# A hybrid decoder block on one core: x tiles in one transfer each, first squares on two engines, six banks for the first transposes, the first weight cast on two engines, head bias rows loaded first

## The chip, the cores and the metric

The kernel runs on one core of a Trainium2 chip. A core has five engines that run side by side, each through its own instructions in order: TensorE (PE in the profile, its weight loads PEld), VectorE (DVE), ScalarE (ACT), GpSimd (POOL) and SyncE (SP), which here issues most of the DMA transfers. They wait for each other and for transfers through semaphores. Matrix products are written to PSUM, in banks of 128 partitions by 512 float32; everything else lies in SBUF. The metric is device time in microseconds (us) for one execution; 0.3% of this kernel is 2.4 us.

## The reference

One block on x of 512 rows by 1024 columns, float32:

```python
h = rmsnorm(x, norm1_g)
z = h @ w_in + b_in                      # 1024 x 6656
z_glu, z_rx, z_rg, z_ga, z_gb = split(z)
u = glu(z_glu); u = causal_depthwise_conv(u, 31 taps); u = silu(layernorm(u))
y_a = u @ conv_w_out + conv_b_out
xb = causal_depthwise_conv(z_rx, 4 taps)
hb = rg_lru(xb, lru_wa, lru_ba, lru_wx, lru_bx, lru_lambda)   # 16 heads of 80
y_b = (hb * gelu(z_rg)) @ lru_w_out
x = x + (sigmoid(z_ga) * y_a + sigmoid(z_gb) * y_b) @ w_mix_out
h = rmsnorm(x, norm2_g)
x = x + (silu(h @ ffn_w1) * (h @ ffn_w3)) @ ffn_w2
return rmsnorm(x, norm_f_g)
```

What matters here is the beginning: the root-mean-square norm of x, its transposition, the first products with w_in, and the small parameters (biases, gains, conv taps) that the later steps read as one column per channel.

## The kernel before

Every product is made of three, in the format that the profile calls fp32r: an operand v is split into h (v cast) and l (v - h), and h·h, h·l and l·h are summed. `split_to` makes both parts: a cast, by default on ACT, and a subtraction (`sub`, L118) on DVE or POOL. A weight chunk is 128 x 1024: `load_chunk` (L147) loads it into a `raw` tile, and `emit_chunk` (L166) splits it into an `hl` tile, low part on POOL for most of the w_in chunks.

The first stage is written out by hand for PE, ACT, DVE and SP (`manual_schedule`, L647); POOL's order follows the program. It goes:

- SP loads x as eight tiles of 128 rows by 512 columns (`load_x`, L494): x0 and x1 in two halves each, then the rows of norm1_g and b_in (`load_rows`, L487), two weight chunks, x2 and x3, two more chunks, the other parameter rows (eleven loads) and, last, the head bias rows (`load_head_rows`, L482). Each of SP's loads signals one of eight semaphores in turn and waits until the load eight before it has landed.
- `norm1_rows(t)`: ACT squares each half of tile t and sums along the row (L559, L565), each with a read of the accumulator; DVE puts in mean and epsilon (L560); ACT takes the root (L566); DVE inverts it (L567) and scales both halves (L614).
- `turn_rows(t)`: PE turns the eight 128 x 128 blocks of a tile (L594) into four PSUM banks, block c into bank c mod 4; x0 and x1 fill one set of banks together, x2 and x3 the next. A bank is read only when PE has written all that goes into it.
- `rows_turned(c0, c1)`: PE turns parameter rows into columns, and DVE copies these to `par` (L528). The first call does norm1_g and b_in; the second, later one all others and the head bias rows, which ACT halves into `bh` (L524). In that second call the head rows come first, `bh` next, the other rows after.
- `turned_parts`: for each block, ACT makes h (`h10h` to `h17h`, L602) with the gain as scale, DVE the low part (`h10l` to `h17l`, L603).
- `early_mm`: the first products. `early_mm(0, 0)` (L636) takes h10h, h10l, h11h ... with the high weights first, and the low weights from the eleventh product on.

The first chunk's cast is on DVE (the `vec.tensor_copy` in L166), its low part on POOL. `load_head_rows` clears its tile on POOL (L480) before the loads; POOL reaches that after the low parts of chunks 0, 2 and 3. After the first stage two ACT instructions (L716) halve 24 of the bias columns; in ACT's order they stand before h10h.

SBUF tiles come from pools: `long` (63 slots of 128 x 512), `raws`, `hls`, and `wsums`, three buffers of 128 x 1024 that the FFN weight sums use later. PSUM has two pools, six banks (`bank`) and two (`bank2`).

Of the kernel before, what the change touches and what calls it, by code (L numbers as in the profile page):

```python
# [85 lines left out]
def tile_block(ctx, tc, a, out):  # L86
# [19 lines left out]
    def bank(name):  # L106
        return psum.tile([P, T], F32, tag="mm", name=name)
# [12 lines left out]
    def split_to(h, l, full, eng, copy=act.copy):  # L120

        copy(h, full)  # L122
        last = sub(eng, l, full, h.bitcast(F32))
        if eng is pool_e:
            newest["sub"] = last.ins
        return h, l

    def split(name, full, eng, p_=None, copy=act.copy):
        p_ = p_ or pairt(name)
        return split_to(*p_, full, eng, copy)  # L130
# [19 lines left out]
    def emit_chunk():  # L150
        key, src, kt, cols, where, lo, after = chunks[emitted[0]]
        if emitted[0] not in loaded_raw:
            load_chunk(emitted[0])
        raw = loaded_raw.pop(emitted[0])
        emitted[0] += 1
        n = kt * cols
        rv = raw[:, :n]
        if where == "gate":
            hl = hls.tile([P, 2, 1024], F32R, tag="hl", name=f"hl_{key}")
            h = hl[:, 0, :n]  # L160
            after(rv, h)
# [314 lines left out]

    heads_b = longt("rowsh")

    def load_head_rows():
        pool_e.memset(heads_b[: 2 * NH, :P], 0.0)  # L480
        for g, name in enumerate(("lru_ba", "lru_bx")):
            nc.sync.dma_start(heads_b[g * NH : (g + 1) * NH, :HB], a[name][0].rearrange("(h p) -> h p", p=HB))  # L482

# [3 lines left out]
        nc.sync.dma_start(rowt[b][r : r + m, :P], src)  # L487

    x_nat = a["x"].rearrange("b (t p) d -> p (b t) d", p=P)
    xt = [[longt(f"x{t}{h}") for h in range(2)] for t in range(NT)]  # L490

    def load_x(t):
        for h in range(2):
            nc.sync.dma_start(xt[t][h], x_nat[:, t, h * T : (h + 1) * T])  # L494

# [22 lines left out]

    def rows_turned(c0, c1):
        pt = bank2(f"par_ps{c0}")  # L520
        if c0:
            at = T - 2 * NH
            pe.transpose(pt[:, at:], heads_b[: 2 * NH, :P], ident[: 2 * NH, : 2 * NH])
            act.activation(bh, pt[:HB, at:], AF.Copy, scale=0.5)  # L524
        for c in range(c0, c1, P):
            m = min(P, c1 - c)
            pe.transpose(pt[:, c - c0 : c - c0 + m], rowt[row_at(c)[0]][:m, :P], ident[:m, :m])
        vec.tensor_copy(par[:, c0:c1], pt[:, : c1 - c0])  # L528

    def pc(name, i):  # L530
        return par[:, col[name] + i : col[name] + i + 1]
# [44 lines left out]
    def turn_half(name, rows, gname, dest, hf, bk, some):  # L576
# [10 lines left out]
            last = vec.scalar_tensor_tensor(out=l, in0=ps[:, :256], scalar=g, in1=h.bitcast(F32), op0=ALU.mult, op1=ALU.subtract)  # L587
        return last_h.ins, last.ins

    def turn_rows(t, ps):  # L590

        for c in range(ND):
            at = 256 * (c // 4) + P * (t % 2)
            pe.transpose(ps[c % 4][:, at : at + P], xt[t][c // 4][:, (c % 4) * P : (c % 4 + 1) * P], ident)  # L594

    def turned_parts(hf, ps):
        cs = slice(hf * 256, hf * 256 + 256)
        for c in range(ND):
            g, at = pc("norm1_g", c), 256 * (c // 4)
            p_ = ps[c % 4][:, at : at + 256]  # L600
            h, l = (v[:, cs] for v in h1p[c])
            act.activation(h, p_, AF.Copy, scale=g)  # L602
            vec.scalar_tensor_tensor(out=l, in0=p_, scalar=g, in1=h.bitcast(F32), op0=ALU.mult, op1=ALU.subtract)  # L603
# [6 lines left out]
    def norm1_rows(t, between=lambda: None):  # L610
        junk = [shortt(f"n1j{t}{h}") for h in range(2)]
        r = rstd_of(xt[t], junk)
        for h in range(2):
            vec.tensor_scalar(out=xt[t][h], in0=xt[t][h], scalar1=r, scalar2=None, op0=ALU.mult)  # L614
            if h == 0:
                between()

    HALVES = [slice(0, 256), slice(256, 512)]
    EARLY = 2
# [3 lines left out]
    def early_mm(i, hf):  # L623
        m = EARLY_IN[i]
        if hf == 0:
            early.append((m, w_tiles(f"in{m}", ND, 0), bank(f"z{m}")))
        _, ws, ps = early[i]
        if (i, hf) == (0, 0):

            order = [(m, c) for c in range(5) for m in (0, 1)]  # L630
            order += [(2, 0), (2, 1), (0, 5), (1, 5), (2, 2), (2, 3), (0, 6), (1, 6), (2, 4), (2, 5), (0, 7), (2, 6), (2, 7), (1, 7)]
            xs = parts_of(h1p, HALVES[0])
            for n, (m, c) in enumerate(order):
                (wh, wl), (xh, xl) = ws[c], xs[c]
                l, r = ((wh, xh), (wh, xl), (wl, xh))[m]
                pe.matmul(ps[:, HALVES[0]], l, r, start=n == 0, stop=n == len(order) - 1)  # L636
            return
        mm3(ps[:, HALVES[hf]], ws, parts_of(h1p, HALVES[hf]), lo_last=hf == 0)
# [71 lines left out]

    def b_in(m):
        return pc("b_in", m)

    for m, n in ((GLU, 16), (GB, 8)):
        cols = par[:, col["b_in"] + m : col["b_in"] + m + n]
        act.activation(cols, cols, AF.Copy, scale=0.5)  # L716

    ready = {m: ps for m, _, ps in early}

# [873 lines left out]
```

## Time and profile before

| | us |
|---|---|
| median of 3 runs | 793.22 |
| lowest, highest | 792.25, 794.7 |
| profiled execution | 793.44 |
| its span, first to last instruction | 791.7 |
| PE busy in the span | 780.2 |
| DVE, ACT, POOL busy | 678.0, 475.0, 358.2 |

A row of the timeline gives start, length, engine, line of the kernel, operation, the tiles out<-in, the shape and a count; in brackets stands how long the engine sat idle before it and what ended that. "SPq" is an instruction that issues a transfer. A row of the lists of groups gives, after the count, the busy time in us, the mean of one in ns and the idle time before.

### The profile page before, as it was taken

The page shows a single profiled execution, that of the slowest core. Times are in us where ns is not written, and L with a number is a line of the kernel's source. Part 1 is how long each engine was busy: PE and PEld are TensorE (multiplying, and loading weights), DVE is VectorE, ACT ScalarE, POOL GpSimd, SP SyncE. Part 2 cuts the span into 40 slices and gives each one's busy share as a digit, 9 for nine tenths or more (in the row PEclk, how much of TensorE's full clock was granted, in tenths as well). Part 3 has the DMA queues.
Part 4 walks back from the last instruction along what each step waited for, and adds up shares of the span by engine and source line. Part 5 has one row for each costly group of instructions (what it writes and reads, how often), then busy time and mean ns, then how long its engine had stood idle before and what let it go on. Part 6 is the DMA issues. An engine that isn't in the chain of part 4 may idle for free.

```text
span 791.7 us, 12476 instructions
## 1 busy us (share of the span) xinstructions
PE 780.2 (99%) x4319; PEld 679.4 (86%) x4319; DVE 678.0 (86%) x1059; ACT 475.0 (60%) x697; POOL 358.2 (45%) x350
## 2 busy tenths in 40 slices
PE   8999999999999999999999999999999999999996
PEld 7888888888888888888887798999999999888885
DVE  5389998887989996999799969897877789999957
ACT  7444678966686866565234666544455546556743
POOL 2367877887788999645550481112322222000000
PEclk9999999999999999999999999999999999999999
DMA  7555999989979978989987896578988889878652
GB/s 218 148 162 169 257 257 259 250 233 288 261 224 300 298 226 266 292 276 286 335 276 247 245 284 208 181 250 290 331 304 300 300 300 292 258 240 260 207 172 107
DMA packets 192261, 199.04 MB, mean 251 GB/s; under 512 B 15278, under 2 KB 153926, under 8 KB 192198
## 3 DMA queue, kind: packets, MB, share of 16 engines
q1 hardware_dynamic: 183093, 166.52, 70.1%
q0 software_dynamic: 8960, 31.46, 11.7%
q8 instruction: 34, 0.56, 0.3%
q14 instruction: 30, 0.24, 0.1%
q10 hardware_dynamic: 144, 0.26, 0.1%
HBM read 146.30 MB, written 38.80 MB: 234 GB/s over the span
## 4 chain that ended last, share of the span: by engine, by line
PE 81%; DVE 10%; DMA 4%; ACT 3%; issue 2%; SPq 0%; DVEq 0%; ACTq 0%
PE z L543 36%; PE fr L1347 24%; PE or L1119 13%; PE f L543 3%; PE g L945 2%; PE yb L543 1%; DMA raw_mxt<-mxt 1%; PE fr L1391 1%; DVE hl_co L118 1%; DMA raw_co<-in_conv_w_out_dram 1%; DVE mxws L118 1%; DVE hl_lo L118 1%; DVE hl_mxb L118 1%; DVE sga L1185 1%; DMA mxws<-in_w_mix_out_dram 1%
## 5 line engine op out<-in xcount | busy, mean ns | idle before, releaser
L745 DVE SCALAR_TENSOR_TENSOR cv<-u,par,cv 128x507 f32<-128x507 f32 (+15 forms) x240 | 162.6, 734 | 1.8 <-ACT cv L741 0.9
L118 POOL TENSOR_TENSOR hl_in<-raw_in,hl_in 128x1024 fp32r<-128x1024 f32 x51 | 123.5, 2432 | 51.2 <-ACT hl_in L122 34.5
L118 POOL TENSOR_TENSOR fws<-fws 128x256 f32<-128x256 f32 x120 | 98.3, 821 | 82.0 <-DMA fws<-in_ffn_w_dram 76.0
L389 POOL DMA_DIRECT2D ot<-fwso x21 | 15.4, 733 | 164.7 <-DVE fwso L118 156.4
L1347 PE MATMUL fr<-hs_0h,hl_ft 128*128 128x256 f32 x320 | 59.2, 283 | 0.0
L122 ACT CAST hl_in<-raw_in 128x1024 fp32r<-128x1024 f32 x51 | 52.9, 1050 | 8.4 <-DMA raw_in<-in_w_in_dram 8.4
L118 DVE TENSOR_TENSOR hl_ft<-raw_ft,hl_ft 128x1024 fp32r<-128x1024 f32 x39 | 47.6, 1220 | 6.3 <-ACT hl_ft L122 6.3
L1347 PEld LDWEIGHTS fr<-hs_0h,hl_ft 128*128 128x128 f32 x320 | 50.6, 192 | 0.0
L122 ACT CAST hl_ft<-raw_ft 128x1024 fp32r<-128x1024 f32 x40 | 41.6, 1048 | 13.8 <-PE fr L1347 6.9
L118 DVE TENSOR_TENSOR hl_fb<-raw_fb,hl_fb 128x1024 fp32r<-128x1024 f32 x30 | 37.0, 1232 | 11.2 <-ACT hl_fb L122 11.1
L1347 PE MATMUL fr<-hs_0l,hl_ft 128*128 128x256 f32 x160 | 45.3, 283 | 0.0
L122 ACT CAST hl_fb<-raw_fb 128x1024 fp32r<-128x1024 f32 x30 | 31.6, 1052 | 17.7 <-PE fr L1347 9.1
L543 PE MATMUL z<-h10h,hl_in 128*128 128x512 f32 (+1 forms) x108 | 41.1, 382 | 0.0
L543 PE MATMUL z<-h13h,hl_in 128*128 128x512 f32 (+1 forms) x108 | 40.8, 379 | 0.0
L543 PE MATMUL z<-h14h,hl_in 128*128 128x512 f32 (+1 forms) x108 | 40.8, 379 | 0.0
L543 PE MATMUL z<-h15h,hl_in 128*128 128x512 f32 (+1 forms) x108 | 40.8, 379 | 0.0
L543 PE MATMUL z<-h16h,hl_in 128*128 128x512 f32 (+1 forms) x108 | 40.8, 379 | 0.0
L543 PE MATMUL z<-h11h,hl_in 128*128 128x512 f32 (+1 forms) x108 | 40.8, 379 | 0.0
L543 PE MATMUL z<-h12h,hl_in 128*128 128x512 f32 (+1 forms) x108 | 40.8, 379 | 0.0
L543 PE MATMUL z<-h17h,hl_in 128*128 128x512 f32 (+1 forms) x108 | 40.8, 379 | 0.0
L122 ACT CAST hl_ob<-raw_ob 128x1024 fp32r<-128x1024 f32 (+1 forms) x23 | 23.4, 1018 | 22.9 <-PE or L1119 14.2
L383 POOL TENSOR_TENSOR fws<-fws 128x256 f32<-128x256 f32 x40 | 32.5, 813 | 3.0
(906 smaller groups left out, 2590.9 us busy)
## 6 DMA issues: line engine op xcount, KB each, us to landing
raw_in<-in_w_in_dram SPq DMA_DIRECT2D x52, 512.0 KB
fws<-in_ffn_w_dram SPq DMA_DIRECT2D x40, 512.0 KB
raw_ft<-fs SPq DMA_DIRECT2D x34, 512.0 KB
fs<-fws SPq DMA_DIRECT2D x21, 512.0 KB
ot<-fwso POOLq DMA_DIRECT2D x21, 512.0 KB, 6.0
fwso<-in_ffn_w_dram POOLq DMA_DIRECT2D x40, 256.0 KB, 7.4
fs<-fws POOLq DMA_DIRECT2D x19, 512.0 KB, 5.1
raw_ob<-in_ffn_w_dram SPq DMA_DIRECT2D x33, 256.0 KB
```

The costliest lines, as they stand in the source:

```text
L118: return eng.tensor_tensor(out=o, in0=x, in1=y, op=ALU.subtract)
L122: copy(h, full)
L383: eng.tensor_tensor(out=q11, in0=q22, in1=q11, op=ALU.add)
L389: return queue.dma_start(dest, raw.rearrange("p (m n) -> p m n", n=256))
L543: pe.matmul(ps, l, r, start=i == 0, stop=i == n - 1)
L745: vec.scalar_tensor_tensor(out=acc[:, s:], in0=u[c][:, : T - s], scalar=dw(c, s), in1=acc[:, s:], op0=ALU.mult, op1=ALU.add)
L945: pe.matmul(ps[:HB], head_chunk[0][:ROWS_G, g, h % 2, m, :], ext[h][m][:ROWS_G], start=m == 0, stop=m == 1)
L1119: pe.matmul(banks[i], l_[:, ts], r_, start=start and n == 0, stop=stop and n == 2, skip_group_check=again)
L1185: vec.scalar_tensor_tensor(out=o, in0=ps, scalar=pc("conv_b_out", j), in1=o, op0=ALU.add, op1=ALU.mult)
L1347: pe.matmul(ps[:, HALVES[i]], lw[:, c, :], rx_, start=not (again or i or c or m), stop=bool(i and c == 3 and m == 2), skip_group_check=True,)
L1391: pe.matmul(self.r4[:, HALVES[i]], lw, rx_, start=not (i or c or m), stop=bool(i and c == 3 and m == 2), skip_group_check=True)
```

## The change

It has six edits, all in the first stage. They shift the line numbers of what follows, so a line number here is always one of the kernel before.

1. x0, x1 and x2 are loaded by one transfer each, of 128 x 1024, into the three `wsums` buffers. x3 stays in two halves.
2. For x0 and x1, `first_sums` squares the left half on ACT and the right half on DVE, by a fused multiply-and-sum whose start value and scale put in epsilon and mean; the root then takes both sums. The order on DVE is: sum of x0, scaling of x0's left half, sum of x1, scaling of x0's right half, scaling of x1's halves.
3. The first transposes go to six banks (five of one pool, one of the other); blocks 0 and 3 share a bank, and so do 4 and 7, and PE turns the blocks in the order 0, 3, 1, 2, 4, 7, 5, 6. The first parameter rows are turned between x0's transposes and x1's, and their columns copied on ACT instead of DVE.
4. The first weight chunk is cast half by ACT, before h10h, and half by POOL, before its low part.
5. The clearing for the head bias rows is POOL's first work after the constants, their loads stand before the other eleven, they are turned after the other rows, and `bh` is made last.
6. The scaling of bias columns stands behind the first product and x2's root on ACT.

After the first stage all engines have the same instructions in the same order as before.

```diff
+    def copy_halves(h, full):
+        act.copy(h[:, :T], full[:, :T])
+        pool_e.tensor_copy(h[:, T:], full[:, T:])
...
-            h, l = split_to(hl[:, 0, :n], hl[:, 1, :n], rv, lo, act.copy if emitted[0] > 1 else vec.tensor_copy)
+            h, l = split_to(hl[:, 0, :n], hl[:, 1, :n], rv, lo, act.copy if emitted[0] > 1 else copy_halves)
...
+    pool_e.memset(heads_b[: 2 * NH, :P], 0.0)
+
     def load_head_rows():
-        pool_e.memset(heads_b[: 2 * NH, :P], 0.0)
...
-    xt = [[longt(f"x{t}{h}") for h in range(2)] for t in range(NT)]
+    wide = [wsums.tile([P, 1024], F32, tag="wsum", name=f"x{t}") for t in range(PIECES)]
+    xt = [[w[:, :T], w[:, T:]] for w in wide] + [[longt(f"x{t}{h}") for h in range(2)] for t in range(PIECES, NT)]
 
     def load_x(t):
+        if t < PIECES:
+            nc.sync.dma_start(wide[t], x_nat[:, t, :])
+            return
...
         pt = bank2(f"par_ps{c0}")
-        if c0:
-            at = T - 2 * NH
-            pe.transpose(pt[:, at:], heads_b[: 2 * NH, :P], ident[: 2 * NH, : 2 * NH])
-            act.activation(bh, pt[:HB, at:], AF.Copy, scale=0.5)
         for c in range(c0, c1, P):
             m = min(P, c1 - c)
             pe.transpose(pt[:, c - c0 : c - c0 + m], rowt[row_at(c)[0]][:m, :P], ident[:m, :m])
-        vec.tensor_copy(par[:, c0:c1], pt[:, : c1 - c0])
+        at = T - 2 * NH
+        if c0:
+            pe.transpose(pt[:, at:], heads_b[: 2 * NH, :P], ident[: 2 * NH, : 2 * NH])
+        (vec.tensor_copy if c0 else act.copy)(par[:, c0:c1], pt[:, : c1 - c0])
+        if c0:
+            act.activation(bh, pt[:HB, at:], AF.Copy, scale=0.5)
...
+    def spot(c, ps):
+        return ((c % 4, c // 4 * 256), ((0, 1, 2, 0, 3, 4, 5, 3)[c], c in (3, 7) and 256))[len(ps) == 6]
+
     def turn_rows(t, ps):
-        for c in range(ND):
-            at = 256 * (c // 4) + P * (t % 2)
-            pe.transpose(ps[c % 4][:, at : at + P], xt[t][c // 4][:, (c % 4) * P : (c % 4 + 1) * P], ident)
+        for c in (range(ND), (0, 3, 1, 2, 4, 7, 5, 6))[len(ps) == 6]:
+            b, at = spot(c, ps)
+            at += P * (t % 2)
+            pe.transpose(ps[b][:, at : at + P], xt[t][c // 4][:, (c % 4) * P : (c % 4 + 1) * P], ident)
...
+    def first_sums(t):
+        junk = [shortt(f"n1j{t}{h}") for h in range(2)]
...
+        act.activation(junk[0], xt[t][0], AF.Square, accum_out=ss[:, 0:1])
+        vec.tensor_tensor_reduce(out=junk[1], in0=xt[t][1], in1=xt[t][1], scale=1.0 / D, scalar=EPS, op0=ALU.mult, op1=ALU.add, accum_out=ss[:, 1:2])
+        act.activation(r, ss[:, 0:1], AF.Sqrt, scale=1.0 / D, bias=ss[:, 1:2])
+        return r
...
-        turned = [bank(f"tx0{q}") for q in range(4)]
-        norm1_rows(0)
+        turned = [(bank if q < 5 else bank2)(f"tx0{q}") for q in range(6)]
+        r0 = first_sums(0)
+        vec.reciprocal(r0, r0)
+        scale_half(0, 0, r0)
+        r1 = first_sums(1)
+        scale_half(0, 1, r0)
         turn_rows(0, turned)
-        norm1_rows(1, lambda: rows_turned(0, n_first))
+        vec.reciprocal(r1, r1)
+        scale_half(1, 0, r1)
+        rows_turned(0, n_first)
+        scale_half(1, 1, r1)
         emit_to(1)
         turn_rows(1, turned)
         turned_parts(0, turned)
...
         norm1_rows(2)
         early_mm(0, 0)
+        for m, n in ((GLU, 16), (GB, 8)):
+            cols = par[:, col["b_in"] + m : col["b_in"] + m + n]
+            act.activation(cols, cols, AF.Copy, scale=0.5)
         early_mm(1, 0)
...
+        load_head_rows()
         for i in range(len(parts)):
             if i not in first:
                 load_rows(i)
-        load_head_rows()
```

More of the change, by code (lines that the diff above doesn't have):

```diff
@@ L598, in turned_parts @@
         for c in range(ND):
-            g, at = pc("norm1_g", c), 256 * (c // 4)
-            p_ = ps[c % 4][:, at : at + 256]
+            g = pc("norm1_g", c)
+            b, at = spot(c, ps)
+            p_ = ps[b][:, at : at + 256]
             h, l = (v[:, cs] for v in h1p[c])
@@ L616, in norm1_rows, with scale_half @@
                 between()
+    def first_sums(t):
+        junk = [shortt(f"n1j{t}{h}") for h in range(2)]
+        i = n_stats[0]
+        n_stats[0] += 1
+        ss, r = stats[:, i, :2], stats[:, i, 2:3]
+        act.activation(junk[0], xt[t][0], AF.Square, accum_out=ss[:, 0:1])
+        vec.tensor_tensor_reduce(out=junk[1], in0=xt[t][1], in1=xt[t][1], scale=1.0 / D, scalar=EPS, op0=ALU.mult, op1=ALU.add, accum_out=ss[:, 1:2])
+        act.activation(r, ss[:, 0:1], AF.Sqrt, scale=1.0 / D, bias=ss[:, 1:2])
+        return r
+    def scale_half(t, h, r):
+        vec.tensor_scalar(out=xt[t][h], in0=xt[t][h], scalar1=r, scalar2=None, op0=ALU.mult)
     HALVES = [slice(0, 256), slice(256, 512)]
@@ L712, in b_in @@
         return pc("b_in", m)
-    for m, n in ((GLU, 16), (GB, 8)):
-        cols = par[:, col["b_in"] + m : col["b_in"] + m + n]
-        act.activation(cols, cols, AF.Copy, scale=0.5)
     ready = {m: ps for m, _, ps in early}
```

## The prediction

> **What bounds the kernel now.** I read the page first, for the engine that sets the time, then the busy times by stretch, for where that engine idles, then the chain of waits, for what ends its idle time.
>
> ```profile
> span 791.7 us, 12476 instructions
> ...
> PE 81%; DVE 10%; DMA 4%; ACT 3%; issue 2%; SPq 0%; DVEq 0%; ACTq 0%
> ```
>
> ```profile
> 0.00:10.24 10.24, 7.46 (x42) 6.66 (x42) 3.37 (x13) 6.02 (x17) 0.98 (x7) 1.00 0.80 240
> ...
> 26.00:100.00 74.00, 74.00 (x351) 61.70 (x350) 61.31 (x105) 38.21 (x56) 48.74 (x35) 1.00 0.71 197
> ...
> 430.00:450.00 20.00, 18.63 (x79) 14.41 (x79) 19.17 (x30) 10.33 (x19) 4.97 (x7) 1.00 0.93 294
> ```
>
> In the stretches the columns after the length are PE, PEld, DVE, ACT and POOL busy, then the granted clock. PE is full from 26 us on, and short only before that and around 430 to 450 us, where it lacks 1.4 us and DVE has 19.2 of 20. So the end moves by what PE gains before 26 us, if the rest of the program keeps its order. It does: after the first stage the changed program holds the same instructions in the same order on every engine.
>
> ```profile
> 1.66 4.58 DMA x<-in_x_dram
> ...
> 25.62 0.52 PE par_ps L527 x3
> 26.14 38.44 PE z L543 x192
> ```
>
> The chain starts at the landing of x, and the turning of the parameter rows is its last stop before PE runs dense. Those are the two places that the change touches. The first, in order of time:
>
> ```profile
> 1.09 5.01 PE L511 MATMUL warm<-ones 128*128 128x128 f32 x24 [1.09 <-DVE ones L504]
> ...
> 6.04 0.88 DVE L614 TENSOR_SCALAR x<-x,stats 128x512 f32<-128x512 f32 x2
> 6.26 0.63 ACT L559 ACTIVATE n1j<-x 128x512 f32<-128x512 f32 x1 [0.45 <-DMA x<-in_x_dram]
> ...
> 6.80 0.19 ACT L559 ACTIVATION_READ_ACCUMULATOR n1j<-x 128x1 f32 x1
> 6.99 0.63 ACT L565 ACTIVATE n1j<-x 128x512 f32<-128x512 f32 x1
> ...
> 8.68 0.21 DVE L528 COPY par<-par_ps 128x60 f32<-128x60 f32 x1
> ...
> 8.82 1.18 PE L594 MATMUL tx<-ident,x 128*128 128x128 f32 x8 [0.88 <-DVE x L614]
> 8.93 0.32 ACT L716 ACTIVATE par<-par 128x16 f32<-128x16 f32 x2 [0.88 <-DVE par L528]
> 9.20 0.69 DVE L122 CAST hl_in<-raw_in 128x1024 fp32r<-128x1024 f32 x1
> 9.71 0.47 ACT L602 ACTIVATE h10h<-tx,par 128x256 fp32r<-128x256 f32 x1 [0.47 <-PE tx L594]
> 9.97 2.38 POOL L118 TENSOR_TENSOR hl_in<-raw_in,hl_in 128x1024 fp32r<-128x1024 f32 x1 [8.66 <-DVE hl_in L122]
> 10.08 0.47 ACT L602 ACTIVATE h11h<-tx,par 128x256 fp32r<-128x256 f32 x1
> ...
> 12.55 0.28 PE L636 MATMUL z<-h10h,hl_in 128*128 128x256 f32 x1
> ```
>
> The first half of tile x1 lands at 6.24 us, the second by 6.99. h10h starts at 9.71 and ends at 10.18; from then on ACT makes one part every 0.37 us, which PE follows. At 12.55 PE first needs the low weights, which POOL finished at 9.97 + 2.38 = 12.35.
>
> **Term 1, the way to h10h.** Let T be the landing of all of x1, by 6.99 us in before. The new x1 is one transfer.
>
> ```profile
> 0.75 1.82 SPq L494 DMA_DIRECT2D x<-in_x_dram  x4
> ```
>
> ```profile
> 0.00:5.40 5.40, 4.31 (x20) 4.31 (x21) 0.38 (x3) 3.04 (x7) 0.71 (x6) 1.00 0.56 176
> 5.40:8.00 2.60, 1.97 (x15) 1.50 (x14) 1.20 (x4) 2.08 (x7) 0.00 (x0) 1.00 1.02 304
> ```
>
> Four issues take 1.82 us, so two issues fewer put the last one 0.91 us earlier: T lies between 6.99 (the engines set it; their share is 1.02 at 5.4 to 8 us) and 6.08 (the issues set it; the share is 0.56 before that). A third of the way, T = 6.7, since the same megabyte has to pass. The squares of x1 now go half to ACT, half to DVE.
>
> ```profile
> L1515 DVE TENSOR_TENSOR of<-x2b,gfh 128x512 f32<-128x512 f32 x4 | 2.8, 690 | 0.1
> ...
> L122 ACT CAST hs_0h<-hs 128x512 fp32r<-128x512 f32 x4 | 2.5, 622 | 4.5 <-DVE hs L118 4.5
> ...
> L209 POOL CAST hl_gate<-raw_gate 40x320 fp32r<-40x320 f32 x8 | 3.9, 489 | 0.5
> ...
> L839 DVE SCALAR_TENSOR_TENSOR xb<-th,xb 128x512 f32<-128x512 f32 x10 | 15.0, 1500 | 4.8 <-DMA th<-tg 4.8
> ...
> L839 DVE SCALAR_TENSOR_TENSOR th<-ea,gr 128x512 f32<-128x512 f32 x10 | 6.8, 682 | 2.4 <-ACT ea L960 2.4
> ```
>
> No fused multiply-and-sum is in the trace. Its price lies between 0.69 us (the two-operand product of that size) and 0.69 + 0.19 (plus an accumulator read as on ACT); the program has the read as an instruction of its own, so I take 0.85. ACT's half takes 0.73, so Sqrt starts at T + 0.85, as the old small addition (0.15) is gone. But h10h does not hang on Sqrt: DVE has the scaling of x0's second half queued behind the new sum. It runs 0.48, until T + 1.33; PE's four transposes behind it take 0.11 each, then comes the row transpose (0.27 to its end), T + 2.05; then, new on ACT ahead of h10h, the parameter copy, 0.2 as on DVE, T + 2.3; then the half cast, 0.62 less the 0.1 by which ACT's next instruction starts early: h10h starts at T + 2.8 = 9.5. The other way, over Sqrt, reciprocal and x1's scaling, took 1.1 from the last square's end (6.99 + 0.73) to x1's first transpose at 8.82; here that is T + 1.95, or T + 2.1 with the reciprocal behind x0's scaling, and two transposes later, T + 2.4, the first bank is ready. The old four banks were ready after five transposes, so this way got shorter, but ACT now comes later than it. Gain 0.2 us.
>
> Ends: T = 6.99 gives 9.8 (a loss of 0.1). With T = 6.08, x0 is the limit: in before its first scaling ended at 6.04 + 0.44 = 6.5, and DVE takes x1's sum behind that, so h10h comes at 9.3 (a gain of 0.4). The first weights have to be there for the half cast at T + 2.3 = 9.0; in before they were by 9.20, when DVE took them without waiting. At that bound h10h slips to 9.7 (no gain).
>
> POOL's half cast: 0.49 us for 320 elements makes about 0.78 for 512. It has until the fifth part, 1.5 us after the first product, so it is hidden; the low weights then begin when both halves are done, about 9.6, and end at 12.0 against a need at 12.55 - 0.2 = 12.35. If the weights land only at 9.20, they end at 12.4, when PE is no earlier than before: no stall to speak of. DVE loses a cast of 0.69 and a copy of 0.21 which nothing on the path waited for.
>
> **Term 2, the middle.** The scaling of the bias columns (0.32 us on ACT, hidden in the idle time before 9.71) moves behind the Sqrt of x2, into ACT's busiest stretch.
>
> ```profile
> 17.10 1.91 PE L594 MATMUL tx<-ident,x 128*128 128x128 f32 x16
> 17.20 0.88 DVE L614 TENSOR_SCALAR x<-x,stats 128x512 f32<-128x512 f32 x2
> ...
> 17.99 4.77 POOL L118 TENSOR_TENSOR hl_in<-raw_in,hl_in 128x1024 fp32r<-128x1024 f32 x2 [5.63 <-DMA rows<-in_norm_g_dram]
> ```
>
> Behind it are x3's squares, its scaling (ready 17.68) and PE's transposes of x3 from 17.10 + 8 x 0.11 = 17.98: 0.3 us of cover for 0.32, a loss of at most 0.1; I take 0.05. POOL's low weights (the first done at 17.99 + 2.4 = 20.4, needed 16 products of 0.12 after the transposes, at 20.8) have 0.4 of cover. x2, now one transfer, is needed only for this stretch; the buffers that x0 to x2 borrow are wanted again after 26 us.
>
> **Term 3, the parameter rows.**
>
> ```profile
> 17.21 2.19 SPq L487 DMA_DIRECT2D rows<-in_conv_dw_w_dram  x3
> ...
> 22.70 0.20 POOL L480 MEMSET rowsh<- 32x128 f32 x1
> ...
> 23.28 0.42 SPq L482 DMA_DIRECT2D rowsh<-in_lru_bx_dram  x1
> ...
> 24.48 0.28 PE L543 MATMUL z<-h17h,hl_in 128*128 128x256 f32 x1
> ...
> 25.03 0.21 PE L523 MATMUL par_ps<-ident,rowsh 32*128 32x32 f32 x1 [0.27 <-DMA rowsh<-in_lru_bx_dram]
> 25.38 0.18 ACT L524 ACTIVATE bh<-par_ps 80x32 f32<-80x32 f32 x1
> ...
> 25.92 0.36 PE L543 MATMUL z<-h10h,hl_in 128*128 128x256 f32 x1
> ```
>
> The clearing sat on POOL behind the low weights, SP waited for it, PE waited for the rows, and the three other transposes waited until ACT had read their bank. A dense product follows after 0.12, as a transpose does (1.91 / 16), so PE would have gone on at 24.60; it went on at 25.92. After the change four transposes run through, 0.4 us together: a gain of 1.32 - 0.4 = 0.9. The clearing (0.2) now stands before the identity is built, done by 1.6 and used after 6. SP's two issues (0.3 and 0.4) go past the eleven row loads; the last of these slips from 19.4 to about 20.1, with some 4 us left until PE turns it. The weight loads behind SP's old wait start some 3 us earlier; no step before 26 us uses them. Ends: 0.8 (one more step of 0.12 to refill PE) and 1.0 (the three old transposes took only 25.92 - 25.62 = 0.3 with the refill, so four may too).
>
> **Sum.** 0.2 - 0.05 + 0.9 = 1.05 us. The profiled execution took 793.44 (791.7 of span, 1.7 around it): 792.4. It was 0.22 above the median shown, 793.22, so the median should be about 792.1.
>
> **Rivals.** A, only the rows pay: the weights or a lock eat term 1. The lock: in the rows above the same DVE form takes 682 ns on one pair of tiles and 1500 on another, and the long ones of these lie under POOL's subtractions. Here POOL's half cast could take the path just before DVE scales x1's first half, if the weights land within T + 1.3 to T + 1.5; that scaling then starts up to 0.78 late and h10h 0.4 late. 793.22 - 0.9 + 0.05 + 0.2 = 792.6. [...]
>
> B, absorbed: from 430 to 450 us DVE sets PE's waits (19.2 of 20 busy) behind transfers. If those keep their absolute time, PE arrives 1 us earlier and waits 1 us longer: 793.2. Against it: that DVE work takes what PE made, so its start moves too.
>
> C, slower: the clock. PE idles after warming up, from about 6.7 until x0's second half is scaled at 8.1. The warm-up ran 24 halves in 5.01 us, 0.21 each, where a transpose later takes 0.12.
>
> ```profile
> 788.00:790.40 2.40, 0.00 (x0) 0.00 (x0) 0.04 (x1) 0.27 (x1) 0.00 (x0) 1.00 0.58 219
> ```
>
> If the clock fell and 5 us passed until it was back, about 22 products from 9.5 to 14.5 would cost 0.12 more each, 2.6 us: 792.1 + 2.6 = 794.7. It decides from the point where the idle time is long enough; at the end of the run the clock still stood at 1.00 through 2.4 us without any PE work. [...]
>
> D, more: x lands at the early bound, 791.9 or less.
>
> **Chances.** Forecast 0.55, A 0.18, B 0.12, C 0.05, D 0.10. The three runs shown spread over 2.4 us, which no term here explains and which the later transfers may shift again, so I give each case about 1.2 us to both sides: 790.4 to 793.8. What a measurement of this kernel tells from no change is about 0.3%, 2.4 us. The forecast and D pass it only with the scatter: faster 0.18; slower is half of C and something unnamed, 0.06; same 0.76.
>
> **What would show it.** Term 1: h10h near 9.5 and ACT's half cast right before it without a wait for the weights; wrong if the first product comes after 10.2 or the fused sum takes over 1 us. Term 2: PE without a gap between 16.8 and 20. Term 3: four row transposes in a row without idle time, the next product 0.4 us later. B shows as longer PE waits at 430 to 450 us; C as a granted clock under 1.00 between 7 and 15. If PE's dense stretch starts 1 us earlier and the end doesn't, the sum was right and the way to the end wrong.

## The result, and the profile after

In the first set the changed kernel took 790.98 us (median of 7 runs, 790.44 to 792.6) beside 794.37 us for the kernel before (7 runs, 792.25 to 794.72), a ratio of 0.9969, 95% interval 0.9957 to 0.998. That is 2.5 us, between 1.6 and 3.4 (0.31% of 794.37; the interval's ends likewise). In a later set 792.37 us (12 runs) stood beside 794.39 (35 runs), 0.9974 (0.9958 to 0.999): 2.1 us, between 0.8 and 3.3. The forecast was 1.05 us. The median of three runs on which it was built, 793.22, was itself 1.2 us under the median of the 35.

The profiled execution took 791.03 us. The page of the changed kernel, span and chain of waits, and its busy times by stretch (columns as before):

```profile
span 789.2 us, 12466 instructions
...
PE 95%; DMA 2%; ACT 1%; DVE 1%; issue 0%; ACTq 0%; DVEq 0%
```

```profile
0.00:8.99 8.99, 7.22 (x42) 6.36 (x42) 3.64 (x13) 4.87 (x13) 1.72 (x9) 1.00 0.83 259
26.00:100.00 74.00, 74.00 (x344) 61.20 (x342) 62.72 (x107) 39.21 (x59) 50.02 (x37) 1.00 0.66 184
430.00:450.00 20.00, 19.01 (x87) 15.00 (x86) 19.17 (x32) 11.98 (x23) 7.07 (x9) 1.00 0.86 262
```

The chain of this execution runs through PE for 95% of the span in place of 81%, with 2% for transfers. That is no measure of the change: the second profile of the changed kernel, below, has 76%, and the kernel before with the parameter rows alone 94%. The first dense product comes at 8.99 us; in the kernel before it was

```profile
10.24 0.38 PE L636 MATMUL z<-h10h,hl_in 128*128 128x256 f32 x1 [0.24 <-ACT h10h L602]
```

The way to it, in the timeline of the changed kernel (its own line numbers: L640 is the fused sum on DVE, L645 the scaling, L609 the transposes, L536 the parameter copy, L129 ACT's half cast, L618 the h parts, L665 the first products):

```profile
4.07 0.69 DVE L640 CUSTOM_DVE_ANT_0 n1j<-x 128x512 f32<-128x512 f32 x1 [3.04 <-DMA x<-in_x_dram]
...
5.39 0.49 DVE L645 TENSOR_SCALAR x<-x,stats 128x512 f32<-128x512 f32 x1
...
5.79 0.69 DVE L640 CUSTOM_DVE_ANT_0 n1j<-x 128x512 f32<-128x512 f32 x1
...
7.73 1.09 PE L609 MATMUL tx<-ident,x 128*128 128x128 f32 x8
7.83 0.21 ACT L536 COPY par<-par_ps 128x60 f32<-128x60 f32 x1 [0.96 <-PE par_ps L532]
...
7.94 0.62 ACT L129 CAST hl_in<-raw_in 128x512 fp32r<-128x512 f32 x1
...
8.46 0.48 ACT L618 ACTIVATE h10h<-tx,par 128x256 fp32r<-128x256 f32 x1
...
8.99 0.39 PE L665 MATMUL z<-h10h,hl_in 128*128 128x256 f32 x1 [0.17 <-ACT h10h L618]
```

x1 is there at 5.42 (its last completion in the record of landings), but DVE takes its sum at 5.79, when x0's left half is scaled. From there it is 2.67 us to h10h. The turning of the parameter rows, in the same timeline:

```profile
23.27 0.28 PE L553 MATMUL z<-h17h,hl_in 128*128 128x256 f32 x1
...
23.39 0.46 PE L532 MATMUL par_ps<-ident,rows 128*128 128x128 f32 x3
...
23.78 0.24 PE L535 MATMUL par_ps<-ident,rowsh 32*128 32x32 f32 x1
...
23.96 0.39 PE L553 MATMUL z<-h10h,hl_in 128*128 128x256 f32 x1
```

From the last product to the next there are now 0.69 us (23.27 to 23.96) in place of 1.44 (24.48 to 25.92), with no wait. Put side by side, the first product is 1.25 us earlier; the last product before the rows 1.21 (24.48 to 23.27); the first after them 1.96 (25.92 to 23.96); the mix stage starts 1.94 earlier (412.22 to 410.28) and the last product of all 2.57 (785.01 to 782.44). So in this pair of executions the way to h10h gave 1.2, the rows 0.75, and a last 0.6 appeared in the mix stage, where the change does nothing.

### The profile page after: what moved, and what is told of

It is laid out like the page before. It is cut to its first block, busy times and chain, and to the rows that moved or that the text cites. A ratio compares the mean times of both kernels' runs of the same rounds, so it can differ in the third digit from the quotient of the medians.

```text
span 789.2 us, 12466 instructions
## 1 busy us (share of the span) xinstructions
PE 779.6 (99%) x4319; PEld 679.2 (86%) x4319; DVE 677.8 (86%) x1059; ACT 473.5 (60%) x695; POOL 358.5 (45%) x351
## 4 chain that ended last, share of the span: by engine, by line
PE 95%; DMA 2%; ACT 1%; DVE 1%; issue 0%; ACTq 0%; DVEq 0%
PE z L553 36%; PE fr L1382 24%; PE or L1154 13%; PE yb L553 7%; PE ya L553 6%; PE f L553 3%; PE mxr L1154 2%; PE g L980 2%; DMA x<-in_x_dram 1%; DMA raw_fb<-in_ffn_w_dram 1%; PE fr L1426 1%; DVE x L1103 0%; PE th L593 0%; PE z L665 0%; PE tx L609 0%; ACT hl_fb L122 0%
```

## The experiments

Theory: two gains that simply add, an earlier first product because x1 lands earlier and its sums are shared, and 0.75 us at the rows. Rivals: the landing was a matter of this one execution; or one of the edits does it all; or the weights, the next transfer, take the gain back. Every kernel but those named is the changed one with one edit; line numbers in the fences are those of the kernel profiled.

### How x lands

The tiles x0 to x2 in halves again, all else as changed:

```diff
-            nc.sync.dma_start(wide[t], x_nat[:, t, :])
+            for h in range(2):
+                nc.sync.dma_start(xt[t][h], x_nat[:, t, h * T : (h + 1) * T])
```

> The changed kernel, but x0 to x2 come in two transfers of 512 columns each again (2 KB runs, six transfers where there were three), into the same buffers. My theory: the first stage gained by the landing of x1 alone (5.4 us in the changed kernel, 7.0 before), so x1's right half lands at about 6.9 again, h10h starts 2.7 us later at about 9.6 (8.46 in the changed kernel), and the kernel loses 1.0 to 1.2 us against the changed one: a profiled span of 790.3. Rival: the new order on DVE and ACT brought the gain and the landing is an accident of one run: h10h stays at 8.4 to 8.7 and the span at 789.2.

Measured: 792.85 us (10 runs), ratio to the kernel before 0.9981 (0.9964 to 0.9999). x1 landed at 6.45, the first product came at 9.96:

```profile
6.63 0.68 DVE L641 CUSTOM_DVE_ANT_0 n1j<-x 128x512 f32<-128x512 f32 x1
...
8.91 0.62 ACT L129 CAST hl_in<-raw_in 128x512 fp32r<-128x512 f32 x1
...
9.44 0.47 ACT L619 ACTIVATE h10h<-tx,par 128x256 fp32r<-128x256 f32 x1
...
9.96 0.38 PE L666 MATMUL z<-h10h,hl_in 128*128 128x256 f32 x1 [0.31 <-ACT h10h L619]
```

From the sum of x1 to h10h it is 2.81 us, as the prediction had it (T + 2.8). So the chain was right, and what differs from the changed kernel is when it starts. The loss of 1.0 to 1.2 us that was expected can't be read from the times (a ratio of 0.9981 beside 0.9969 and 0.9974 of the changed kernel), nor from single executions: the changed kernel's first product came at 8.99 in one and at 10.26, later than here, in the other, shown below. Two more kernels ask whether the number of transfers or the length of a contiguous run decides: halves of 64 rows by 1024 (runs of 4 KB, four transfers for x0 and x1), and x0 with x1 in two transfers of both tiles' left and both tiles' right halves (runs of 2 KB).

```diff
-            nc.sync.dma_start(wide[t], x_nat[:, t, :])
+            for g in range(2):
+                nc.sync.dma_start(wide[t][64 * g : 64 * g + 64], x_nat[64 * g : 64 * g + 64, t, :])
```

> The changed kernel with each of x0 to x2 in two transfers of 64 rows of 1024 columns: as many transfers as before, but runs of 4 KB. If the length of the runs sets the landing, x1 is there at 5.3 to 5.7 us and h10h starts before 8.8. If the number of issues sets it, x1 lands near 6.9 and h10h starts near 9.6.

```diff
-    wide = [wsums.tile([P, 1024], F32, tag="wsum", name=f"x{t}") for t in range(PIECES)]
+    both = hls.tile([P, 2, 1024], F32R, tag="hl", name="x01")
+    both = both.rearrange("p t n -> p (t n)").bitcast(F32)
+    wide = [both[:, :1024], both[:, 1024:], wsums.tile([P, 1024], F32, tag="wsum", name="x2")]
...
-            nc.sync.dma_start(wide[t], x_nat[:, t, :])
+            if t == 2:
+                nc.sync.dma_start(wide[t], x_nat[:, t, :])
+            else:
+                nc.sync.dma_start(both.rearrange("p (t n) -> p t n", t=2)[:, :, t * T : (t + 1) * T], x_nat[:, :2, t * T : (t + 1) * T])
```

> The changed kernel with x0 and x1 in two transfers of 512 KB, as the changed kernel has, but the first takes the left halves of both tiles and the second the right halves, so the runs are 2 KB. If the number of issues sets the landing, the second has landed by 5.4 to 5.7 us (read at the start of DVE's first sum, which takes a right half); if the runs set it, near 6.9. The way from there to h10h is longer than in the changed kernel, since x0's sum can't start before, so the time of the whole says nothing here.

Measured: four transfers with long runs landed x1 at 7.75 us, two with short runs at 5.88. So the run doesn't decide: 5.88 with 2 KB lies within the 5.42 to 6.00 that two transfers gave with 4 KB, and 4 KB gained nothing with four. That fewer transfers land earlier stands; that their issues set the landing isn't shown, and the 6.9 expected of four was missed. Transfers of 256 KB are issued 0.46 us apart, but land 1.05 apart on average (four executions), those of 512 KB 1.34 apart (eight). In the 64-row kernel, with 0.64 us from issue to issue, the DMA engines are busy (share 1.02 from 4 to 5 us) and move less (201 GB/s, where the changed kernel has a share of 0.93 and 330 GB/s).

The first kernel took 796.53 us, over all runs of the changed one, the second 793.24, within them (one run each). In both the first products were late for another reason too: PE sat idle for 1.98 us (5.59 to 7.57) in the first, for 1.25 and 0.69 us in the second, and the granted clock fell, as the busy times by stretch show (the number before the last two is the clock), first those of the 64-row kernel, then those of the paired one:

```profile
7.00:8.00 1.00, 0.43 (x3) 0.46 (x4) 0.58 (x2) 0.16 (x1) 0.00 (x0) 0.90 1.12 247
8.00:14.00 6.00, 5.40 (x24) 4.45 (x23) 4.20 (x12) 4.26 (x13) 2.98 (x2) 0.50 1.09 262
14.00:15.00 1.00, 1.00 (x8) 1.00 (x7) 1.00 (x3) 1.00 (x2) 0.00 (x0) 0.69 1.07 337
```

```profile
10.00:11.00 1.00, 1.00 (x7) 1.00 (x8) 0.07 (x1) 0.96 (x3) 0.08 (x1) 0.70 1.04 391
11.00:12.00 1.00, 1.00 (x5) 0.67 (x4) 0.83 (x3) 1.00 (x4) 1.00 (x1) 0.50 1.08 349
12.00:14.00 2.00, 2.00 (x11) 2.00 (x11) 2.00 (x7) 2.00 (x6) 1.30 (x1) 0.55 1.17 292
```

Read by its shares, with 1.00 and 0.50 as the only values (an estimate from these rows), the clock was at half for 0.2 + 6 + 0.6 = 6.8 us in the one (0.90 of 1 us, 0.50 of 6, 0.69 of 1) and 0.6 + 1 + 1.8 = 3.4 us in the other. x1's eight transposes took 1.97 and 1.57 us in place of 1.09, and the stretch from the first to the last product before the rows 15.16 us (12.00 to 27.16) and 14.54 (11.19 to 25.73) in place of 14.28. That is rival C, in kernels where all of x0 is there only at 5.51 and 5.88 us, for 4.04 in the changed one.

### Does the landing repeat?

The kernel before and the changed one, profiled once more, unchanged.

> The kernel before, unchanged, profiled a second time, to see how much the profiled execution itself varies. If the earlier landing of the changed kernel belongs to its transfer plan, the second tile of x lands at 6.9 to 7.0 us again (within 0.3 us) and the first product starts near 10.2 us; if it was a matter of the single execution, the landing moves by 0.5 us or more. If the half microsecond that the changed kernel gained in the mix stage belongs to the edits, the idle stretches of TensorE in that stage add up to about 1.35 us again; if it varies by itself, they add up to something else by 0.3 us or more.

> The changed kernel, unchanged, profiled and timed again. Theory: as in the kernels that differ from it little, the second tile of x lands at 5.8 to 5.9 us, not at 5.42 us, the sum of the second tile begins at 6.2 to 6.35 us when VectorE has scaled the first half of the first tile, and the first product comes at 9.4 to 9.6 us, 0.7 us before the kernel before and not 1.25; the rows stage gives 0.8 us; the time 1.5 to 2.0 us below the kernel before in systematic terms, and what lies beyond that comes from single idle stretches that both kernels show in some executions. Rival: the landing at 5.42 us and the first product at 9.0 us come again, and the time is 2.5 us or more below.

The kernel before: 794.67 us (one run); x1 at 6.56, 0.4 earlier than the first time, which lies between the two cases that were to be told apart, but the first weights at 9.85, and the first product waits for them:

```profile
9.29 0.47 ACT L602 ACTIVATE h10h<-tx,par 128x256 fp32r<-128x256 f32 x1 [0.47 <-PE tx L594]
...
9.87 0.69 DVE L122 CAST hl_in<-raw_in 128x1024 fp32r<-128x1024 f32 x1 [1.00 <-DMA raw_in<-in_w_in_dram]
...
10.71 0.36 PE L636 MATMUL z<-h10h,hl_in 128*128 128x256 f32 x1 [1.13 <-DVE hl_in L122]
```

In the mix stage PE waits 0.6 us for DVE, where it waited 1.3 the first time: that stage varies by itself. The changed kernel: x1 at 6.00, its sum at 6.38, and the weights only at 9.19. ACT's half cast waits for them and h10h stands behind it:

```profile
9.21 0.62 ACT L129 CAST hl_in<-raw_in 128x512 fp32r<-128x512 f32 x1 [0.58 <-DMA raw_in<-in_w_in_dram]
...
9.74 0.47 ACT L618 ACTIVATE h10h<-tx,par 128x256 fp32r<-128x256 f32 x1
...
10.26 0.38 PE L665 MATMUL z<-h10h,hl_in 128*128 128x256 f32 x1 [0.85 <-ACT h10h L618]
```

So in this execution the first product is no earlier than the 10.24 of before: rival A in its first form. The landing at 5.42 was an early one, and the theory's 9.4 to 9.6 for the first product fell too, to the later side.

### The cast, the sums and the banks

The first cast whole on DVE, as before, and its half on DVE with POOL keeping the other:

```diff
-            h, l = split_to(hl[:, 0, :n], hl[:, 1, :n], rv, lo, act.copy if emitted[0] > 1 else copy_halves)
+            h, l = split_to(hl[:, 0, :n], hl[:, 1, :n], rv, lo, act.copy if emitted[0] > 1 else vec.tensor_copy)
```

> The changed kernel with the first weight cast on DVE as a whole again. My theory: the half cast on ACT (0.62 us, between the parameter copy and h10h) stands on the path, since DVE is idle from 8.0 to 9.0; so h10h starts about 0.4 us earlier, near 8.1, the first product follows the DVE cast at about 8.7 instead of 9.0, and PE's dense stretch starts 0.1 to 0.3 us earlier. Rival: the split of the cast is worth its 0.3 us because the low weights wait for DVE's whole cast: first product at 9.0 or later.

```diff
-        act.copy(h[:, :T], full[:, :T])
+        vec.tensor_copy(h[:, :T], full[:, :T])
```

> The changed kernel with ScalarE's half of the first cast given to VectorE, which is idle there; GpSimd keeps the other half. Theory: ScalarE's half cast of 0.62 us stands ahead of h10h, and without it h10h waits for its two transposes alone: 0.3 us sooner behind VectorE's sum of the second tile (2.35 us after that sum begins, where the changed kernel took 2.67 and 2.80 us), the first product and all that follows it 0.2 to 0.4 us earlier at an equal landing. Rival: the landing of the weights (7.9 to 8.8 us) or GpSimd's half bounds the first product, and it moves by less than 0.1 us.

With the whole cast on DVE (792.2 us, one run) h10h comes 2.48 us after x1's sum (6.35 to 8.83), 0.2 sooner than with ACT's half ahead of it. But the weights landed at 8.84 here and bound the first product, 9.70, so what it is worth at equal weights stays open. With DVE's half (792.41 us, 12 runs, ratio to before 0.9971, 0.9955 to 0.9986) h10h comes 2.47 after the sum (6.25 to 8.72), 0.2 sooner than as changed, where 0.3 was expected. Yet the product gained almost none of it:

```profile
8.15 0.77 POOL L130 CAST hl_in<-raw_in 128x512 fp32r<-128x512 f32 x1 [6.71 <-DMA raw_in<-in_w_in_dram]
...
8.36 0.84 DVE L129 CAST hl_in<-raw_in 128x512 fp32r<-128x512 f32 x1
8.72 0.47 ACT L618 ACTIVATE h10h<-tx,par 128x256 fp32r<-128x256 f32 x1 [0.22 <-PE tx L609]
...
9.35 0.36 PE L665 MATMUL z<-h10h,hl_in 128*128 128x256 f32 x1
9.35 2.38 POOL L118 TENSOR_TENSOR hl_in<-raw_in,hl_in 128x1024 fp32r<-128x1024 f32 x1 [0.44 <-DVE hl_in L129]
```

DVE casts a whole chunk in 0.69 us, so some 0.35 as an estimate for half of one, which took 0.84 here: it began under POOL's half and ended 0.28 after it. The first product waits for that, 0.63 behind h10h in place of 0.53, and POOL's low part comes later too: the first low-weight product stands 2.44 us behind the first product (11.79) in place of 2.31 (11.30), and products behind the rows resume 15.16 us after the first one in place of 14.97. Counted from x0's landing (4.49 here, 4.04 as changed) the first product is 0.1 us earlier (4.86 for 4.95), and 0.2 are lost behind it: the rival was right, and no version better than the changed kernel came of it. The paired kernel has the form that the prediction named under A, a scaling under POOL's half cast, 0.84 us in place of 0.48, in its timeline:

```profile
8.20 0.61 POOL L130 CAST hl_in<-raw_in 128x512 fp32r<-128x512 f32 x1 [6.76 <-DMA raw_in<-in_w_in_dram]
...
8.24 0.84 DVE L650 TENSOR_SCALAR x<-x,stats 128x512 f32<-128x512 f32 x1
```

Both squares of a tile on ACT, and the first transposes in four banks, with the old order of the blocks:

```diff
-        vec.tensor_tensor_reduce(out=junk[1], in0=xt[t][1], in1=xt[t][1], scale=1.0 / D, scalar=EPS, op0=ALU.mult, op1=ALU.add, accum_out=ss[:, 1:2])
-        act.activation(r, ss[:, 0:1], AF.Sqrt, scale=1.0 / D, bias=ss[:, 1:2])
+        vec.tensor_scalar(out=ss[:, 0:1], in0=ss[:, 0:1], scalar1=1.0 / D, scalar2=EPS, op0=ALU.mult, op1=ALU.add)
+        act.activation(junk[1], xt[t][1], AF.Square, accum_out=ss[:, 1:2])
+        act.activation(r, ss[:, 1:2], AF.Sqrt, scale=1.0 / D, bias=ss[:, 0:1])
```

> The changed kernel with both halves of the squares of the first two tiles summed on ScalarE, one after the other, and their scaling prepared by a small VectorE instruction between. Theory that the division of the sums pays: the square root of the second tile comes some 0.3 to 0.5 us later after its landing than in the changed kernel (there 6.58 us against a landing at 5.42 us, 1.16 us), and ScalarE's h10h with it (there 3.04 us behind the landing), so 0.2 to 0.5 us at the first product. Rival: VectorE's chain of the first tile bounds this place and is relieved by 0.77 us, so that h10h comes no later, or earlier.

```diff
-        turned = [(bank if q < 5 else bank2)(f"tx0{q}") for q in range(6)]
+        turned = [bank(f"tx0{q}") for q in range(4)]
```

> The changed kernel with the first transposes in four banks, as before, in place of six. Theory: ScalarE's copy of the parameters and its half of the cast stand between the transposes and h10h, so the banks cost nothing: h10h between 2.9 and 3.2 us behind the landing of the second tile, the first product 0 to 0.1 us later. Rival: with two chunks to a bank the first readers wait for the last transposes of their bank, and h10h or the splits behind it come 0.2 to 0.4 us later.

One run each, 792.57 and 791.24 us. Timelines, the one without DVE's sums first:

```profile
8.41 0.62 ACT L129 CAST hl_in<-raw_in 128x512 fp32r<-128x512 f32 x1
...
8.49 1.09 PE L609 MATMUL tx<-ident,x 128*128 128x128 f32 x8 [0.23 <-DVE x L646]
...
9.03 0.47 ACT L618 ACTIVATE h10h<-tx,par 128x256 fp32r<-128x256 f32 x1
```

```profile
8.14 1.09 PE L609 MATMUL tx<-ident,x 128*128 128x128 f32 x8
...
8.35 0.62 ACT L129 CAST hl_in<-raw_in 128x512 fp32r<-128x512 f32 x1
...
9.01 0.47 ACT L618 ACTIVATE h10h<-tx,par 128x256 fp32r<-128x256 f32 x1
```

x0 landed at 4.485 and 4.457 here, at 4.04 in the changed kernel's first profile. Counted from there, x1's transposes start after 4.01 us without DVE's sums, 3.68 with four banks, 3.69 as changed; h10h after 4.55, 4.55 and 4.42 (4.42 also in the kernel with the rows late, below). So the shared sums save 0.33 us at the transposes, but only 0.13 of it is left at h10h, since ACT's half cast stands there; the two added banks are worth 0.13 there. Counted from x1's landing, as the expectations do, h10h comes after 3.25 without DVE's sums, the lower edge of what was expected, and after 3.19 with four banks, its upper one.

### One edit at a time on the kernel before

The x tiles alone (edit 1):

> The kernel before with one part of the change alone: the first three tiles of x in one transfer each. Theory: the second tile lands at 5.4 to 5.9 us in place of 6.6 to 7.0 us, but the squares of both tiles still stand one after the other on ScalarE, so that its last square begins only some 0.2 to 0.4 us earlier than before (there 6.98 and 6.58 us in the two profiled executions) and the first product 0.1 to 0.5 us earlier; the rows stage and the time: 0.1 to 0.5 us below the kernel before. Rival: the landing alone is what counts and the other parts of the way are hidden, so that the first product comes 0.9 us or more earlier and the time is 1 us or more below.

Measured: 794.57 us (12 runs), ratio 1.0003 (0.9986 to 1.0019). x1 landed at 5.67 and the first product came at 9.70, 0.54 before that of the kernel before, a little more than expected. In the timeline, and in the list of what PE waited for (us in total, number of waits, the longest):

```profile
6.46 0.61 ACT L569 ACTIVATE n1j<-x 128x512 f32<-128x512 f32 x1
...
8.28 1.18 PE L598 MATMUL tx<-ident,x 128*128 128x128 f32 x8 [0.26 <-DVE x L618]
...
9.17 0.47 ACT L606 ACTIVATE h10h<-tx,par 128x256 fp32r<-128x256 f32 x1 [0.47 <-PE tx L598]
...
9.70 0.39 PE L640 MATMUL z<-h10h,hl_in 128*128 128x256 f32 x1 [0.24 <-ACT h10h L606]
```

```profile
PE mxr L1123 <- DVE x L1072: 2.3, 4, 1.2
...
PE mxr L1123 <- DVE sga L1189: 0.8, 1, 0.8
```

ACT squares four halves in a row, the last begins at 6.46, and from x0's landing (4.26) to the first product it takes 5.44 us where the changed kernel takes 4.95. The half microsecond won was lost again, and more, between 414 and 451 us, where this execution waits 3.1 us for DVE against 1.3 in the first profile of before (line L1119 there). The kernel that starts its mix stage earliest, the changed one in its first profile, waits 1.2 there, so this is scatter rather than an answer to an earlier start; the table below gives it a size.

The parameter rows alone (edit 5, with the order in `rows_turned` as in the change), and the changed kernel without that edit:

```diff
+    pool_e.memset(heads_b[: 2 * NH, :P], 0.0)
     def load_head_rows():
-        pool_e.memset(heads_b[: 2 * NH, :P], 0.0)
...
+        load_head_rows()
         for i in range(len(parts)):
             if i not in first:
                 load_rows(i)
-        load_head_rows()
```

> The kernel before with the change of the parameter rows alone: the two halvings of bias columns stay behind the products, so that what is moved is the load of the head rows, its memset and the order of the transposes. Theory: first product as before (10.2 to 10.8 us), idle TensorE time at the rows stage down from 0.59 to 0.69 us and its first ready product 0.7 to 0.9 us nearer to the first product, the time 0.7 to 0.9 us below the kernel before. Rival: the mix stage takes it up, and the time is within 0.3 us of before.

> The changed kernel with the parameter rows as they were: head rows loaded after the other rows, their transpose ahead of the others. Theory: the way to the first product is untouched, and the 0.8 us that the rows stage gained in the trace are lost, so that products behind that stage resume near 24.8 us instead of 24.0 us and the time is 0.7 to 0.9 us above the changed kernel's, 791.7 to 791.9 us. Rival: the shorter wait is only passed on, and the mix stage takes it up, so that the end moves by less than 0.3 us.

Measured: 793.42 us for the rows alone (12 runs, 0.9993, 0.9972 to 1.0015) and 792.99 for the change without them (10 runs, 0.9976, 0.9954 to 0.9998). The times can't tell 0.8 us; the timelines can. The rows alone, then the change without them:

```profile
24.50 0.28 PE L545 MATMUL z<-h17h,hl_in 128*128 128x256 f32 x1
...
25.18 0.39 PE L545 MATMUL z<-h10h,hl_in 128*128 128x256 f32 x1
```

```profile
24.50 0.21 PE L531 MATMUL par_ps<-ident,rowsh 32*128 32x32 f32 x1 [0.44 <-DMA rowsh<-in_lru_bx_dram]
...
25.00 0.52 PE L535 MATMUL par_ps<-ident,rows 128*128 128x128 f32 x3 [0.28 <-ACT bh L532]
...
25.31 0.36 PE L551 MATMUL z<-h10h,hl_in 128*128 128x256 f32 x1
```

From the last product to the next it is 0.69 us with the edit and 1.52 (23.79 to 25.31) without it, whatever the other edits are. Edits 2, 3 and 4 were not run alone on the kernel before, and edit 6 in no run by itself; what each is worth there stays open.

### All executions together

From the trace of each profiled execution: landing of x1 and of the first weights, start of the first product, time from the last product before the rows to the next, from there to the mix stage's first product, and from that to the last product of the program.

| kernel | x1 | weights | first product | rows | to mix | mix to end |
|---|---|---|---|---|---|---|
| before | 6.97 | 8.78 | 10.24 | 1.44 | 386.30 | 372.79 |
| before, again | 6.56 | 9.85 | 10.71 | 1.44 | 387.99 | 371.68 |
| before + rows | 6.99 | 8.78 | 10.26 | 0.69 | 386.33 | 372.29 |
| before + x tiles | 5.67 | 8.02 | 9.70 | 1.44 | 386.45 | 374.96 |
| changed | 5.42 | 7.86 | 8.99 | 0.69 | 386.33 | 372.16 |
| changed, again | 6.00 | 9.19 | 10.26 | 0.69 | 386.33 | 372.55 |
| x in halves | 6.45 | 8.89 | 9.96 | 0.69 | 386.34 | 373.26 |
| x in 64 rows | 7.75 | 10.79 | 12.00 | 0.69 | 387.93 | 372.33 |
| x in pairs | 5.88 | 8.14 | 11.19 | 0.69 | 386.33 | 371.86 |
| cast on DVE | 5.91 | 8.84 | 9.70 | 0.69 | 386.33 | 372.46 |
| half cast on DVE | 5.80 | 8.09 | 9.35 | 0.69 | 386.83 | 373.08 |
| sums on ACT | 5.78 | 8.34 | 9.56 | 0.69 | 387.73 | 371.71 |
| four banks | 5.82 | 8.14 | 9.53 | 0.69 | 386.33 | 371.84 |
| rows late | 5.88 | 8.28 | 9.51 | 1.52 | 386.44 | 371.91 |

The rows are the same to 0.01 us in all ten executions with edit 5. The last two columns follow no edit: one wait of 1.1 to 1.4 us near 190 us came in three executions, of before and of two variants of the change, and from the mix stage on they spread over 3.3 us. A straight line through the fourteen (least squares) has the last product 0.89 us earlier for each microsecond that the mix stage starts earlier, with a standard error of 0.17: an earlier start is passed on, whole or nearly so.

## Why the prediction was right, and where it was short

**The place and the kind** were right: PE is full behind 26 us (74.00 us busy of 74 from 26 to 100 us, in both kernels' first profiles) but for 430 to 450 (18.63 and 19.01 of 20), the two touched places give the gain, and it reaches the end.

**Term 1, the way to h10h**, forecast 0.2 us: the mechanism was right, and the term was mis-sized at T, the landing of x1. It was put at 6.7, "a third of the way, since the same megabyte has to pass", between 6.99 and 6.08. With two transfers of 128 rows x1 landed at 5.42 to 6.00 in the eight executions with the change's load of x, 5.78 on average, below even the early end; with the old halves at 6.45 to 6.99, 6.74 on average, in four. The difference, 0.96, is close to the 0.91 us of issuing from which the prediction had its early bound, which was hung on one late execution. So the reason given for staying near 6.99, that the same megabyte has to pass, failed: the bytes are the same, and in two transfers they are there earlier. That it is the issuing that does it is not shown, as the 64-row kernel says. The next limit was the one named for the early end of T, x0's chain on DVE, but it stood at 5.79 (up to 6.38 in the other executions), not at 6.5: x0's squares no longer stand one behind the other, and the fused sum took 0.69 and a read of 0.08, 0.77 for 0.85. From that start to h10h the prediction said 2.8 and the runs 2.67 (changed) and 2.81 (x in halves). POOL's half cast took 0.61 for 0.78.

The gain at the first product isn't one number. Over the three executions with the old way (before twice, before + rows) it starts at 10.40 on average, over the three with the new way (changed twice, rows late) at 9.59: 0.8 us, between none and 1.7 for single pairs. Where the weights land later than about 9.2 (an estimate: the first product stood 1.07 behind them, 10.26 - 9.19), as in one of these three, rival A holds.

**Term 2**, forecast -0.05: from the first product to the last before the rows 14.24 us before, 14.28 and 14.29 after. Right.

**Term 3**, forecast 0.9 (0.8 to 1.0): 0.75. The wait went as described; the four transposes were taken for 0.4 us and need 0.57 (23.39 to 23.96), as three take 0.13 each and the last 0.18.

**The sum.** What the traces support is 0.8 - 0.05 + 0.75, about 1.5 us against 1.05 forecast. The ratios give 2.5 (1.6 to 3.4) and 2.1 (0.8 to 3.3); 1.5 lies just under the first interval and within the second. That 790.98 is inside the range of 790.4 to 793.8 says little: the range is 3.4 us wide, three times the forecast gain. The 0.6 us more that the first pair of profiles showed lies in the mix stage and is within its spread; whether a part of it is systematic stays open. The times alone can't settle it: the kernel before ranged from 791.45 to 797.13 in one set.

**Rivals.** A occurs in single executions. What it calls a lock was not seen on the changed kernel's path: in its first profile DVE scales x1's halves from 7.11 us, 0.88 for the two, and POOL's half cast begins at 7.92. In two other kernels a DVE instruction beside that half cast took longer: 0.84 us in place of 0.48 for the scaling in the paired one, and 0.84 in place of an estimated 0.35 for the half cast on DVE. Why, no run shows; a lock is the author's guess. The prediction's own evidence for it, 1500 against 682 ns, compares unlike things: the form of 682 ns takes its second input from PSUM (`gr`), and it keeps its length under POOL's subtractions (0.68 us, 105.57 to 106.25, inside one from 104.43 to 106.84), while the long ones, 1.49 to 4.03 us under such subtractions, take both inputs from SBUF. B falls as a whole, since the end follows the start of the mix stage by 0.89 us in one; that a tenth is absorbed there is not excluded. C did not happen, and was not as remote as the end of the run made it look: in the 64-row kernel the clock fell to 0.50 behind 1.98 us without a product, so an early x0 may be what keeps it away; no run tests that. The prediction has it decided by the length of the idle time, and the runs show no one length that does (the last section). By the measured time D was the nearest (791.9 or less, a chance of 0.10), and x1 landed earlier than even D had it; that the first pair of profiles lay 2.57 us apart owes 0.6 to the mix stage, by luck as far as is known.

## What to carry to other kernels

When data land at the start of a kernel can depend on the number of transfers that bring them: the same megabyte was there 0.96 us earlier in two than in four. A bound for it should come from several executions, since this one moved by 0.6 us between runs of the same load. An edit of a microsecond in one of 800 is judged from the distance between two marks in the trace (0.69 us in all ten executions with edit 5, 1.44 to 1.52 in the four without), not from the time, whose scatter is several times larger (791.45 to 797.13 for the kernel before). Work that no longer bounds the way leaves the next limit right behind it: here the weights' landing, by which the changed kernel lost its first 1.25 us in the second execution.

## What was not expected of the hardware

The granted clock fell to 0.50 after an idle stretch of 1.98 us, and in another kernel after 1.25 and 0.69 us of idle time with 0.63 us of transposes between; with 0.70, 0.54 and 1.13 us of idle time the second profile of before kept 1.00 (8 to 14 us). At the end of the kernel before, the last product is over at 785.40 and the clock stays at 1.00 until about 790.5 (0.55 from 790.40 to 791.70): 5.1 us without a product. So no one length of idle time decides here. What does was not shown.

Four transfers of 64 rows by 1024 landed x1 1.3 us later than four of 128 rows by 512 (7.75 against 6.45, one execution each), with as many bytes and runs twice as long. They were issued 0.64 us apart for 0.46, which makes 0.5 of it; the rest is open.
